# Dilated 3x3 convolution: pair 0 in one transfer beside the weights, and six pairs asked for ahead instead of five

## The chip, the cores and the metric

The kernel runs on one core of a Trainium2 chip. The metric is the device time of one execution in microseconds; the time before is the median of three runs. A core has TensorE (PE, with its weight loads PEld), VectorE (DVE), ScalarE (ACT), GpSimd (POOL) and SyncE (SP), and 16 DMA engines that move data between the chip's memory and the core. SyncE, ScalarE and GpSimd can each ask for transfers, each into a queue of its own; all queues are served by the same 16 DMA engines.

## The reference

The inputs are x (16 images, 64 channels, 64 x 64, float32) and weight (128 x 64 x 3 x 3, float32). The dilation is 2 and the padding is 2, so the output is 16 x 128 x 64 x 64 in float32:

```
x_pad = np.pad(x, ((0, 0), (0, 0), (pad, pad), (pad, pad)))
for b, co, ci, kh, kw:
    output[b, co] += weight[co, ci, kh, kw] * x_pad[b, ci, kh*2:kh*2+64, kw*2:kw*2+64]
```

## The kernel before

**Tiling.** Two images form a pair: their 2 x 64 channels fill the 128 partitions, one row of 64 x 64 float32 (16 KB) on each. There are eight pairs (NP). On TensorE the two images are two matmuls on 64 partitions each, issued in turn.

**The arithmetic.** With dilation 2 the rows fall into groups of four (a quad): two rows of an even class and two of an odd class (e and r in the code). The three rows of weights w0, w1, w2 are regrouped so that fewer matmuls are needed: the sum of the even and odd classes (s16) is multiplied with w1 once and used for both classes, and the differences w2 - w1 and w0 - w1 (slots w21 and w01) and w0 and w2 complete each class. Each pair is done in four units (u) of four quads. A unit has three phases of matmuls: w1 on s16, which ScalarE copies out of PSUM (line 204), and two class phases, which VectorE adds to that copy and writes to the output tile (line 209). The PSUM pool has four buffers.

**Loads.** Pair 0 comes as float32 in two pieces of rows (0 to 35, 36 to 63) from SyncE's queue, into x32, which borrows a slot of the output pool (three slots). VectorE (line 130, rows 0 to 19) and ScalarE (line 132, the rest) convert it to float16, and GpSimd forms s16 from it directly (line 141, `prepare`). All other pairs come through GpSimd's queue, which converts to float16 on the way (line 81, `load`); x16 has six slots. The weights come first in SyncE's queue (line 64), ahead of pair 0.

**Weights.** Two ScalarE copies (line 99) convert them, VectorE and GpSimd form w21 and w01 (line 103), 15 small matmuls transpose them (line 117), and VectorE and ScalarE move the transposed blocks from PSUM to w_sb (lines 126 and 128).

**Order.** The order on each engine is the order in which the code issues; there is no scheduler. On GpSimd it is: first half of w01, load of pair 1, second half of w01, sums of rows 0 to 19 of pair 0, loads of pairs 2, 3 and 4, sums of the other rows of pair 0, and from then on the sums of the next pair within the loop, with the loads of pairs 5, 6 and 7 each ahead of the sums of pairs 4, 5 and 6:

```
if u == 1 and AHEAD <= pb + 2 < NP:
    load(pb + 2, [0, H])
```

**Stores.** SyncE's queue stores pairs 0 to 4 whole (line 221), pairs 5 and 6 per image, and pair 7 per image and half (line 224). An output slot is written again three pairs later, after its store.

Of the kernel before, what the change touches and what calls it, by code (L numbers as in the profile page):

```python
# [10 lines left out]
def kernel(  # L11
# [7 lines left out]
    nc = tc.nc  # L19

    B, CI, H, W = x.shape
# [38 lines left out]
    x_pair = x.rearrange("(nb two) c h w -> nb (two c) h w", two=2)  # L60


    w32 = wpool.tile([CO, CI * NK], f32, name="w32")
    nc.sync.dma_start(out=w32, in_=weight.rearrange("o i h w -> o (i h w)"))  # L64

    x16 = {}
    s16 = {}
# [3 lines left out]
    cuts0 = [0, 20, 36, 52, H]  # L71
    x32 = opool.tile([P, 2, H, W], f32, tag="o", name="x32")[:, 0]
    x16[0] = x16pool.tile([P, H, W], f16, tag="x16", name="x16_0")
    for lo, hi in ((0, 36), (36, H)):
        nc.sync.dma_start(out=x32[:, lo:hi], in_=x_pair[0, :, lo:hi])


    def load(pb, cuts):
        x16[pb] = x16pool.tile([P, H, W], f16, tag="x16", name=f"x16_{pb}")
        for lo, hi in zip(cuts, cuts[1:]):  # L80
            nc.gpsimd.dma_start(out=x16[pb][:, lo:hi], in_=x_pair[pb, :, lo:hi])  # L81

    AHEAD = 5


    zero = wpool.tile([P, NB], f16, name="zero")
# [13 lines left out]
    for name, a in (("w21", 2), ("w01", 0)):  # L100
        for u in range(2):
            eng = nc.vector if name == "w21" else nc.gpsimd
            eng.tensor_sub(  # L103
                out=w16[:, SLOT[name] * KW : (SLOT[name] + 1) * KW, u, :],
# [8 lines left out]
    for n, name in enumerate(("w1", "w21", "w0", "w01", "w2")):  # L113
        ps = cpool.tile([P, 2, NB], f32, tag="ps", name=f"wt{n}")
        k0 = SLOT[name] * KW
        for j in range(KW):
            nc.tensor.matmul(  # L117
                out=ps[:, 0, j * CO : (j + 1) * CO],
# [16 lines left out]
    def prepare(pb, lo, hi):  # L135
        if pb not in s16:
            s16[pb] = sumpool.tile([P, 2 * NQ, W], f16, tag="s16", name=f"s16_{pb}")
        src = (x16[pb] if pb else x32).rearrange("p (q e r) w -> p q e (r w)", e=2, r=2)
        dst = s16[pb].rearrange("p (q r) w -> p q (r w)", r=2)
        q0, q1 = lo // 4, hi // 4  # L140
        nc.gpsimd.tensor_add(  # L141
            out=dst[:, q0:q1], in0=src[:, q0:q1, 0, :], in1=src[:, q0:q1, 1, :]
        )

    prepare(0, 0, 20)
    for pb in range(2, AHEAD):
        load(pb, [0, H])
# [42 lines left out]
    for pb in range(NP):  # L190
        o = opool.tile([P, 2, H, W], f32, tag="o", name=f"o{pb}")
        ov = o.rearrange("p b (q e r) w -> p b q e (r w)", e=2, r=2)
        for u in range(NU):

            if u == 1 and AHEAD <= pb + 2 < NP:
                load(pb + 2, [0, H])
# [8 lines left out]
            for e, terms in enumerate(  # L205
# [4 lines left out]
                    out=ov[:, :, u * UQ : (u + 1) * UQ, e, :],  # L210
# [49 lines left out]
```

## Time and profile before

| | |
|---|---|
| median of three runs | 126.11 us (126.09 to 126.12) |
| profiled execution, first to last instruction (span) | 124.3 us |
| PE busy | 105.2 us (85% of the span) |
| VectorE busy | 80.8 us (65%) |
| GpSimd busy | 41.4 us (33%) |
| ScalarE busy | 39.6 us (32%) |
| read from and written to the chip's memory | 17.07 MB, 33.55 MB |
| weights, issue to landing | 2.9 us |
| pair 0, its two pieces, issue to landing | 6.5 and 10.6 us |
| other pairs, issue to landing, median of seven | 16.0 us |

The page gives the profiled execution by its span; the runs' time holds 1.8 us more than the span, before the first and after the last instruction. In the lists of groups, a line names the source line, the engine, the operation, the tiles out<-in, the shapes, and the number of instructions. The slices cut the span in 40 parts of 3.1 us, and their digits are tenths of busy time. The DMA row is the mean over the 16 DMA engines, and the GB/s are bytes written: a load that converts float32 to float16 writes half of what it reads. "SPq" and "POOLq" are the queues' issuing instructions.

### The profile page before, as it was taken

Reading aid. Unit: us, or ns where it says so; the run is one execution under the profiler, and the core shown is the slowest. Engines: PE = TensorE matmul, PEld = TensorE weight load, DVE = VectorE, ACT = ScalarE, POOL = GpSimd, SP = SyncE. Lnnn points to the kernel's source line nnn. Section 1 sums busy time; section 2 is a strip of 40 time slices with the busy share of each in tenths; the row PEclk is TensorE's granted clock in tenths of the full one; section 3 lists DMA queues with packets and bytes.
Section 4 is the critical chain, followed back from the end, with each engine's and each line's share of the span. In section 5 each row is a group of like instructions: output and inputs, shape, how many; then the busy total and the mean of one; then the engine's idle time right before and its main releaser. Section 6 shows DMA issues by size and latency. Waiting matters only on the chain.

```text
span 124.3 us, 2244 instructions
## 1 busy us (share of the span) xinstructions
PE 105.2 (85%) x981; PEld 55.7 (45%) x981; DVE 80.8 (65%) x71; ACT 39.6 (32%) x40; POOL 41.4 (33%) x33
## 2 busy tenths in 40 slices
PE   6357999999999999999999999999999999960000
PEld 2043555555555555555555555555555555520000
DVE  0470199787778777877769778777877787770000
ACT  4760823333333333333333333333332433320000
POOL 2859998794095009500930093000000000000000
PEclk9999999999999999999999999999999999999655
DMA  4999999999999999999999999999999999999991
GB/s 129 346 359 218 214 214 216 224 237 411 393 327 314 332 306 319 316 390 314 324 345 427 425 427 432 422 427 427 432 438 427 432 414 432 427 417 419 422 406 71
DMA packets 3961, 43.42 MB, mean 349 GB/s; under 512 B 368, under 2 KB 368, under 8 KB 624
## 3 DMA queue, kind: packets, MB, share of 16 engines
q1 hardware_dynamic: 2944, 35.95, 68.9%
q0 software_dynamic: 1008, 7.34, 28.4%
q8 instruction: 7, 0.11, 0.3%
q14 instruction: 2, 0.02, 0.0%
HBM read 17.07 MB, written 33.55 MB: 407 GB/s over the span
## 4 chain that ended last, share of the span: by engine, by line
PE 80%; DMA 5%; POOL 2%; DVE 1%; DVEq 1%; SPq 0%; issue 0%
PE ps L186 80%; DMA x<-in_x_dram 5%; POOL s L141 2%; DVE o L209 1%; DVEq L255 1%; SPq L64 0%; DVEq L209 0%
## 5 line engine op out<-in xcount | busy, mean ns | idle before, releaser
L209 DVE TENSOR_TENSOR o<-ps,s 128x1024 f32<-128x1024 f32 x64 | 76.7, 1223 | 25.9 <-PE ps L186 16.8
L186 PE MATMUL ps<-x,w_sb 64*128 64x496 f16 (+3 forms) x768 | 85.3, 368 | 0.0
L186 PEld LDWEIGHTS <-w_sb 64*128 64x128 f16 x960 | 53.4, 95 | 49.3 <-issue 3.7
L204 ACT COPY s<-ps 128x1024 f32<-128x1024 f32 x32 | 32.4, 1012 | 63.0 <-PE ps L186 63.0
L141 POOL TENSOR_TENSOR s<-x 128x1152 f16<-128x1152 f16 (+4 forms) x18 | 35.1, 1971 | 31.1 <-PE ps L186 28.3
L186 PE MATMUL ps<-s,w_sb 64*128 64x496 f16 (+1 forms) x192 | 26.5, 379 | 2.1 <-POOL s L141 2.1
L81 POOL DMA_DIRECT2D x<-in_x_dram x7 | 4.0, 579 | 0.0
L132 ACT CAST x<-x 128x1024 f16<-128x1024 f32 (+1 forms) x3 | 2.8, 973 | 3.4 <-DMA x<-in_x_dram 3.4
L93 PE MATMUL warm<-zero 128*128 128x512 f16 x6 | 2.7, 630 | 1.2 <-DVE zero L87 1.2
L117 PE MATMUL wt<-ident,w 128*128 128x128 f16 x15 | 1.8, 312 | 2.1 <-ACT w L99 2.1
L103 DVE TENSOR_TENSOR w<-w 128x192 f16<-128x192 f32 x2 | 1.5, 800 | 2.5 <-DMA w<-in_weight_dram 2.5
L117 PEld LDWEIGHTS <-w 128*128 128x128 f16 x15 | 1.5, 146 | 3.0 <-ACT w L99 3.0
L99 ACT CAST w<-w 128x576 f16<-128x576 f32 x2 | 2.3, 1222 | 1.6 <-DMA w<-in_weight_dram 1.6
L103 POOL TENSOR_TENSOR w<-w 128x192 f16<-128x192 f32 x2 | 1.9, 951 | 2.4 <-DMA w<-in_weight_dram 2.4
L126 DVE CAST w_sb<-wt 128x384 f16<-128x384 f32 x3 | 1.6, 552 | 1.4 <-PE wt L117 1.4
L93 PEld LDWEIGHTS <-zero 128*128 128x128 f16 x6 | 0.7, 138 | 2.3 <-DVE zero L87 1.2
L99 ACT ACT_TABLE_LOAD x1 | 1.3, 1283 | 0.7 <-PEq L241 0.7
L128 ACT CAST w_sb<-wt 128x384 f16<-128x384 f32 x2 | 1.0, 478 | 1.1 <-PE wt L117 1.1
L130 DVE CAST x<-x 128x1280 f16<-128x1280 f32 x1 | 0.8, 826 | 0.5 <-DMA x<-in_x_dram 0.5
L87 DVE MEMSET zero<- 128x256 uint32 x1 | 0.3, 272 | 0.9 <-PEq L241 0.9
masks.py:199 POOL TENSOR_SCALAR_AFFINE_SELECT ident<-ident 128x128 f16<-128x128 f16 x1 | 0.3, 292 | 0.1
masks.py:197 POOL MEMSET ident<- 128x128 f16 x1 | 0.2, 204 | 0.3 <-POOLq L241 0.3
(4 smaller groups left out, 0.4 us busy)
## 6 DMA issues: line engine op xcount, KB each, us to landing
out_dram<-o SPq DMA_DIRECT2D x5, 4096.0 KB, 21.6
out_dram<-o SPq DMA_DIRECT2D x4, 2048.0 KB, 12.4
x<-in_x_dram POOLq DMA_DIRECT2D x7, 1024.0 KB, 16.0
out_dram<-o SPq DMA_DIRECT2D x4, 1024.0 KB, 10.6
x<-in_x_dram SPq DMA_DIRECT2D x1, 1152.0 KB, 6.5
x<-in_x_dram SPq DMA_DIRECT2D x1, 896.0 KB, 10.6
w<-in_weight_dram SPq DMA_DIRECT2D x1, 288.0 KB, 2.9
```

Source lines behind the costliest of these rows:

```text
L81: nc.gpsimd.dma_start(out=x16[pb][:, lo:hi], in_=x_pair[pb, :, lo:hi])
L93: nc.tensor.matmul(out=warm[:, 0], lhsT=zero[:, 0:P], rhs=zero, start=True, stop=True)
L99: nc.scalar.copy(out=w16[:, 0:NK, u, :], in_=w32k)
L103: eng.tensor_sub(out=w16[:, SLOT[name] * KW : (SLOT[name] + 1) * KW, u, :], in0=w32k[:, a * KW : (a + 1) * KW, :], in1=w32k[:, KW : 2 * KW ...
L117: nc.tensor.matmul(out=ps[:, 0, j * CO : (j + 1) * CO], lhsT=w16[:, k0 + j, :, :].rearrange("o t i -> o (t i)"), rhs=ident, start=True, st ...
L126: nc.vector.tensor_copy(out=dst, in_=ps[:, 0, 0 : KW * CO])
L132: nc.scalar.copy(out=x16[0][:, lo:hi], in_=x32[:, lo:hi])
L141: nc.gpsimd.tensor_add(out=dst[:, q0:q1], in0=src[:, q0:q1, 0, :], in1=src[:, q0:q1, 1, :])
L186: nc.tensor.matmul(**m)
L204: nc.scalar.copy(out=s32, in_=phase(pb, u, [("w1", 2, 0)]))
L209: nc.vector.tensor_add(out=ov[:, :, u * UQ : (u + 1) * UQ, e, :], in0=ps.rearrange("p b (q c) -> p b q c", c=QW), in1=s32.rearrange("p b ( ...
L255: with _tile.TileContext(nc) as tc:
```

## The change

The weights are asked for from ScalarE's queue instead of SyncE's. Pair 0 is one transfer of 64 rows per partition (2 MB) instead of two of 36 and 28 rows, and stands first in SyncE's queue. AHEAD goes from 5 to 6: the load of pair 5 follows those of pairs 2, 3 and 4 ahead of the first unit, and the loop loads only pairs 6 and 7. The cuts in which pair 0 is converted and summed stay.

```
     w32 = wpool.tile([CO, CI * NK], f32, name="w32")
-    nc.sync.dma_start(out=w32, in_=weight.rearrange("o i h w -> o (i h w)"))
+    nc.scalar.dma_start(out=w32, in_=weight.rearrange("o i h w -> o (i h w)"))
...
     x16[0] = x16pool.tile([P, H, W], f16, tag="x16", name="x16_0")
-    for lo, hi in ((0, 36), (36, H)):
-        nc.sync.dma_start(out=x32[:, lo:hi], in_=x_pair[0, :, lo:hi])
+    nc.sync.dma_start(out=x32, in_=x_pair[0])
...
-    AHEAD = 5
+    AHEAD = 6
```

## The prediction

> **What bounds the kernel now.** I read the page's slices first, for what runs without a break; then the chain that ended last, the issues of transfers with their landings, GpSimd's timeline, and the start in stretches of half a microsecond. From the page:
>
> ```profile
> span 124.3 us, 2244 instructions
> ...
> PE   6357999999999999999999999999999999960000
> ...
> DMA  4999999999999999999999999999999999999991
> ...
> HBM read 17.07 MB, written 33.55 MB: 407 GB/s over the span
> ```
>
> Two resources run nearly the whole time: PE from slice 6 to 36, and the 16 DMA engines from slice 2 to the end. The packet records of the trace bear out the second: first packet at 1.74 us, last at 122.6, and the packets' durations add up to 121.3 us per engine, so there is no idle DMA time to win. The span is 124.3 us; the median of the runs, 126.11, is 1.8 above it, which I take as constant around the span. I sum shifts of the span's end and add them to 126.11.
>
> ```profile
> 1.17 6.48 DMA x<-in_x_dram
> 7.65 0.07 issue
> 7.72 2.19 POOL s L141
> ...
> 9.95 99.61 PE ps L186 x948
> ...
> 109.66 1.23 DVE o L209
> ```
>
> The chain: the first piece of pair 0 lands at 7.65, GpSimd adds its rows, PE starts at 9.95 and doesn't stop. The chain stops at VectorE, 12 us before the end: behind it are only stores, which still drain. The issues, from the page, last column issue to landing:
>
> ```profile
> x<-in_x_dram SPq DMA_DIRECT2D x1, 1152.0 KB, 6.5
> x<-in_x_dram SPq DMA_DIRECT2D x1, 896.0 KB, 10.6
> w<-in_weight_dram SPq DMA_DIRECT2D x1, 288.0 KB, 2.9
> ```
>
> The weights, first in SyncE's queue, land at 0.74 + 2.9 = 3.6. GpSimd's timeline shows what hangs on them:
>
> ```profile
> 3.69 1.10 POOL L103 TENSOR_TENSOR w<-w 128x192 f16<-128x192 f32 x1 [2.38 <-DMA w<-in_weight_dram]
> 4.74 0.70 POOL L81 DMA_DIRECT2D x<-in_x_dram  x1
> 5.46 0.80 POOL L103 TENSOR_TENSOR w<-w 128x192 f16<-128x192 f32 x1
> 7.72 2.18 POOL L141 TENSOR_TENSOR s<-x 128x640 f16<-128x640 f32 x1 [1.47 <-DMA x<-in_x_dram]
> 9.84 1.63 POOL L81 DMA_DIRECT2D x<-in_x_dram  x3
> ```
>
> The load of pair 1 stands in GpSimd's order behind a subtraction that waits for the weights. Windows of 0.5 us (last columns: DMA share, GB/s written):
>
> ```profile
> 7.50:8.00 0.50, 0.32 (x3) 0.15 (x2) 0.32 (x1) 0.46 (x2) 0.28 (x1) 1.00 1.09 459
> 8.00:8.50 0.50, 0.00 (x0) 0.00 (x0) 0.50 (x2) 0.50 (x2) 0.50 (x1) 1.00 1.39 408
> 8.50:9.00 0.50, 0.00 (x0) 0.00 (x0) 0.50 (x3) 0.46 (x1) 0.50 (x1) 1.00 0.94 180
> ```
>
> The rate halves at 8.5: loads that convert write half of what they read. The first of their packets starts at 8.24, 3.5 us after the issue at 4.74, and just as most engines finish pair 0. That hand-over has no gap.
>
> **The change, part by part.** *Pair 0 in one transfer.* Removed: one issue on SyncE (0.42 us), 128 packets. Each DMA engine carries 8 rows: 8 x (0.347 + 0.272) = 4.95 us now, 8 x 0.611 (the stores' packet of a whole 16 KB row) = 4.89 after: 0.06 saved. But rows 0 to 19 are now usable only when all rows have landed.
>
> *Weights on ScalarE's queue.* Their issue (0.37) goes ahead of, or behind, the table load (0.74 to 2.02). ScalarE idles 1.62 us before its first weight copy, so the issue costs nothing by itself, but the order "weights, then x" is gone; both transfers use the same 16 engines. How two queues share an engine the trace shows where the slowest two engines still hold rows of pair 0 while conversion loads are queued: their 7 KB packets start at 9.28, 10.16 and 11.05, steps of 0.88 to 0.89 = 0.272 + 0.624, one packet of each in turn. The weights are 8 packets of 0.093 per engine; in turn with 0.611 they need eight steps, 8 x 0.704 = 5.63 us, as long as pair 0 itself. From 1.74 that is 7.4. Slow packets add 0.84 (means now 126, 411 and 280 ns against medians 93, 347 and 272, times 8), so 8.2; the slowest engine was 1.3 later in the first piece (last packet 6.99 against some 5.6), so 9.5; landing followed the last packet by 0.35. Pair 0 lands at 9.9, the weights one row earlier, at **9.2 instead of 3.6**. Bounds: 3.6 (all weight packets first) and 9.9 (behind the rows).
>
> *What the weights hold up.* GpSimd's order stays: subtraction, issue of pair 1 at weights + 1.13, first packet 3.5 later, 9.2 + 4.63 = 13.8. For those 3.5 there are two rows: this one, and 4.6 for the load of pair 5 (28.77 to 33.34) beside stores; I take the first, the same instruction in the same place, and keep both. DMA engines finish pair 0 at 8.5 on the mean, the slowest at 9.5 without the interleaving. So they idle 5.3 us on the mean, 4.3 on the slowest. Nothing else can fill this: the next transfer of another queue is the store of pair 0 at 25.45 plus the delay. As no idle DMA time lies behind it, it moves the end. The final semaphores arrived at 123.37 from the slowest engine, and the first below the two slowest at 122.71: 122.71 + 5.3 = 128.0 against 123.37 + 4.3 = 127.7, so **+4.6**, less 0.06.
>
> *PE.* GpSimd finishes its weight work at weights + 2.65 = 11.85, adds the rows in 2.19, and PE starts at 14.1, 4.1 later. The path through ScalarE is shorter: copies 2.34, transposes and VectorE's eviction done 3.5 after the weights. Is a PE that is 4.1 late worse than a DMA that is 4.6 late? The store of pair 6 is issued at 99.75, starts at 101.74, and the one before ends at 101.7: its slack is what exceeds the shortest issue-to-packet time, between 1.0 (first issue) and 2.0, so 0 to 1.0, take 0.5. PE's delay counts 3.6, inside the 4.6.
>
> *Six pairs ahead.* One more issue (0.55) on GpSimd between the first rows and rows 20 to 35: those were ready at 12.75, PE wanted them at 14.54, so 1.8 covers it; without that cover it would cost the 0.55. Pair 5's load moves from the issue at 28.77 to right behind pair 4's. The DMA total is the same, and by 29 stores fill the engines: zero. It delays the first stores, though: VectorE waits once, 1.23 us at 62.5, for the store of pair 1 to free its buffer. Sharing engines half and half, I put that store's end 5.8 later, 1.7 more than PE's delay, so that wait becomes some 2.9. PSUM's four buffers hid 1.23 wholly; up to 1.0 may reach PE, 4.1 + 1.0 - 0.5 = 4.6: the same end.
>
> Sum: 126.11 + 4.6 - 0.06 = **130.7**.
>
> **Rivals.** *Weights get through first.* If ScalarE's transfer reaches the engines some 0.4 us ahead (one issue's length), three or four packets go alone, and the weights land near 5.9; in one go, at 3.6. Then conversion loads start between 8.2 and 10.5, the DMA gap shifts the end by at most 122.71 + 2.0 - 123.37 = 1.3, and pair 0's landing rules: 9.9 + 0.07 + 2.2 = 12.2, PE 2.2 late, less 0.5 of slack: +1.7, **127.8**. For it: the two engines leave the opening barrier together. Against: SyncE's first issue starts as early as any (0.74), and alternating from the start already gives my case. The Trainium skill, DMA: Bandwidth & Descriptors, section "Queues, rings and completion order", says that an engine drains a whole packet, typically 9 to 17 descriptors, before it turns to another queue. By that rule all eight weight rows would pass in one go, landing at 3.6 or behind pair 0 at 9.9, for 127.8 or 131.4; the steps of 0.88 us above speak for one row at a time.
>
> *A gain in the slowest engine (the other side).* The lag of 1.3 us arises among the slow packets of the first 7 us. If one transfer of whole rows had none, and the weights passed early, all would land at 1.74 + 5.63 + 0.35 = 7.7, PE starts as before, loads follow at 8.24, and the last engine ends up to 1.3 earlier: **124.8**. It decides only if pair 0 lands before 8.2 and the weights before 4.0; the first 2 MB took until 8.5 even on the mean engine. The Trainium skill's section "Anatomy of one DMA — SWDGE (gpsimd) path" on the same page gives each transfer a fixed cost of about 2.0 us. By it one transfer less would land pair 0 2.0 us sooner, an estimate from that page; but the second piece's packets start at 5.91, before the first's last at 6.99, so here nothing fixed stood between them.
>
> *No change:* the landing is hidden, with pair 0 at 8.5 (mean engine) and the weights by 4: PE starts at 10.8, 0.8 late, which the upper bound of the slack (1.0) takes in, and loads follow at 8.6: **126.1**.
>
> **How the numbers follow.** Late weights 0.70, weights first 0.20, no change 0.05, gain 0.05. The likeliest has its own range: weights from 7.1 (1.74 + 8 x 0.704 - 0.61 + 0.35, no slow packet) give loads at 11.8 and +2.6, 128.7; weights at 9.9 with 4.6 to the first packet give loads at 15.6 and +6.4, 132.5. With the rival at 127.8 the range is 127.4 to 132.3. What a measurement here can tell from no change is 0.2%, 0.25 us: faster 0.05, same 0.05, slower 0.90.
>
> **What would show it.** Right: GpSimd's and VectorE's waits for the weights grow from 2.4 to some 8 us; pair 1's issue near 10.3; a hole of 4 to 5 us in the DMA slices before 14; PE's first convolution near 14, its run still 99.6 long or up to 1 longer; stores dense to the end. Wrong: weights landed by 6 (then the start is ruled by pair 0 and PE), a DMA hole that other transfers fill, or a tail with idle DMA between the last stores, which would mean that PE and not DMA sets the end.

## The result, and the profile after

The changed kernel takes 131.25 us (131.01 to 131.40), the kernel before 126.12 beside it: a ratio of 1.037, with a 95% interval of 1.0335 to 1.0405. The change costs 5.1 us. The profiled execution took 131.2, with a span of 129.4 against 124.3, so the 1.8 us around the span stayed. Medians are over all executions of a kernel; ranges and ratios leave out those that were disturbed.

The page of the changed kernel (slices of 3.2 us, tenths of busy time):

```profile
span 129.4 us, 2241 instructions
...
PE   6203999999999999999999999999999999950000
...
DMA  4953999999999999999999999999999999999991
...
HBM read 17.07 MB, written 33.55 MB: 391 GB/s over the span
```

The bytes are the same, but the DMA row has a dip at slices 3 and 4, which the row of before lacks: a hole, in which the DMA engines stand idle. Behind it the row is dense to the end, as it was. Windows of the changed kernel over the hole (each line: the stretch and its length, the busy time of PE, PEld, VectorE, ScalarE and GpSimd, the granted clock, and last the DMA share and the GB/s written; before, the DMA share was 1.05, 1.01 and 1.10 in these windows):

```profile
8.00:10.00 2.00, 0.00 (x0) 0.00 (x0) 0.59 (x2) 0.59 (x1) 0.54 (x1) 1.00 0.13 51
10.00:12.00 2.00, 0.20 (x3) 0.20 (x4) 0.92 (x1) 1.75 (x2) 1.98 (x4) 1.00 0.22 25
12.00:14.00 2.00, 2.00 (x19) 1.55 (x19) 1.66 (x2) 1.17 (x3) 2.00 (x3) 1.00 0.82 123
```

The cause stands in the issues and in GpSimd's order. Issues of the changed kernel, last column issue to landing:

```profile
x<-in_x_dram SPq DMA_DIRECT2D x1, 2048.0 KB, 8.4
w<-in_weight_dram ACTq DMA_DIRECT2D x1, 288.0 KB, 8.7
```

GpSimd's timeline of the changed kernel (start, length, engine, line, operation, what ended the idle time before it):

```profile
9.46 1.11 POOL L102 TENSOR_TENSOR w<-w 128x192 f16<-128x192 f32 x1 [8.15 <-DMA w<-in_weight_dram]
10.51 0.70 POOL L80 DMA_DIRECT2D x<-in_x_dram  x1
11.23 0.80 POOL L102 TENSOR_TENSOR w<-w 128x192 f16<-128x192 f32 x1
11.98 1.53 POOL L140 TENSOR_TENSOR s<-x 128x640 f16<-128x640 f32 x1
13.46 2.46 POOL L80 DMA_DIRECT2D x<-in_x_dram  x4
```

The weights, asked for at 0.73, land at 9.38 instead of 3.6, pair 0 lands whole at 9.18, and pair 1's load is issued at 10.51 instead of 4.74. Nothing is left in any queue from 8.7 until that load's first packet at 11.94.

The chain that ended last (start, length, what):

```profile
0.73 8.65 DMA w<-in_weight_dram
...
9.41 2.35 ACT w L98 x2
...
11.80 1.78 PE wt L116 x15
13.59 55.19 PE ps L185 x516
...
68.88 1.24 DVE o L208
...
70.16 43.64 PE ps L185 x420
...
113.89 1.22 DVE o L208
```

The start now runs through ScalarE's weight copies, and there is a break at 68.8: PE waits for a free PSUM buffer, because VectorE waited there. VectorE's timeline shows it:

```profile
68.88 3.48 DVE L208 TENSOR_TENSOR o<-ps,s 128x1024 f32<-128x1024 f32 x3 [2.42 <-PE ps L185]
```

The profile names PE as releaser, but pair 1's store, whose buffer the next output tile takes, has its last landing at 68.76, just before: it was the store.

### The profile page after: what moved, and what is told of

Read it like the earlier page. It is cut to its first block, busy times and chain, and to the rows that moved or that the text cites. A ratio compares the mean times of both kernels' runs of the same rounds, so it can differ in the third digit from the quotient of the medians.

```text
span 129.4 us, 2241 instructions
## 1 busy us (share of the span) xinstructions
PE 105.7 (82%) x981; PEld 56.0 (43%) x981; DVE 81.4 (63%) x71; ACT 39.5 (31%) x40; POOL 41.0 (32%) x33
## 4 chain that ended last, share of the span: by engine, by line
PE 78%; DMA 7%; DVE 2%; ACT 2%; DVEq 1%; issue 0%
PE ps L185 76%; DMA w<-in_weight_dram 7%; DVE o L208 2%; ACT w L98 2%; PE wt L116 1%; DVEq L254 1%; DVEq L208 0%
## 5 line engine op out<-in xcount | busy, mean ns | idle before, releaser
L140 POOL TENSOR_TENSOR s<-x 128x1152 f16<-128x1152 f16 (+4 forms) x18 | 34.4, 1939 | 30.0 <-PE ps L185 28.5
L129 DVE CAST x<-x 128x1280 f16<-128x1280 f32 x1 | 1.4, 1392 | 0.0
```

The costliest lines, as they stand in the source:

```text
L129: nc.vector.tensor_copy(out=x16[0][:, 0:20], in_=x32[:, 0:20])
L140: nc.gpsimd.tensor_add(out=dst[:, q0:q1], in0=src[:, q0:q1, 0, :], in1=src[:, q0:q1, 1, :])
```

## The account of the DMA engines

In the packet records of the trace the durations, summed and divided by the 16 engines, give a busy time. What is left between the first packet (at 1.74 in both) and the end of the last is idle time and the lag of the slowest engine; as records overlap a little, it can come out just below zero. (The prediction's 122.6 is where the last row packet starts; it ends at 122.9.)

| profiled execution | busy | last packet ends | left over |
|---|---|---|---|
| before | 121.3 | 122.9 | -0.2 |
| changed | 122.3 | 128.0 | 4.0 |

Left over is 4.1 us more (0.6 of it before 9 us, 3.4 from 9 to 14), busy 0.9 more, together the 5.1 by which the last packet ends later. The 0.9 is slow packets: pair 1's load, the first behind the hole, averages 712 ns a packet instead of 632 (0.64 us per engine), and the loads of pairs 4 and 5 add 0.54 near 32 us, where the first store joins; pair 0 itself gives 0.14 back. That pair 1's packets are slow because of the hole is not shown: in four runs below that have pair 0 in one transfer and no hole ahead of this load they average 661 to 702.

PE's delay is not what sets the end here. Pair 6's store was issued at 103.91 and its first packet went at 106.67, 2.77 later, while 0.83 is the shortest such time of this store in any run (below): it stood in a queue. PE's last matmul came 4.2 later than before; the DMA engines were later still.

## The experiments

Theory A is that of the prediction: weights in turns with pair 0's rows, a late load of pair 1, and a hole that moves the end. The rivals are the whole-row transfer, the sixth pair, and the late PE. "Before" is the median beside each run, on the same chip.

**Weights first again**, in the changed kernel:

```
-    nc.scalar.dma_start(out=w32, in_=weight.rearrange("o i h w -> o (i h w)"))
+    nc.sync.dma_start(out=w32, in_=weight.rearrange("o i h w -> o (i h w)"))
```

> The changed kernel with the weights put back first in SyncE's queue; pair 0 stays one transfer and six pairs stay ahead. Theory A (the weights, slowed by pair 0's rows, issue pair 1's load late, and the DMA engines stand idle): weights at 3.6, no DMA hole, pair 0 at 8.5 to 9.5, PE from 10.7 to 11.5, time 126.0 to 127.1. Theory B (the whole-row transfer or the sixth pair is what costs): 129 or more.

128.29 (127.35 to 129.04) against 126.53, ratio 1.0135 (1.0065 to 1.0206). The hole is gone (packets of pair 1 from 7.87), and with it some 3 us of the 5.1. But the time is above what theory A expected, and this kernel's chain (start, length, what) shows the whole-row landing:

```profile
1.17 8.34 DMA x<-in_x_dram
...
9.58 2.18 POOL s L140
...
11.80 100.58 PE ps L185 x948
```

So the order of the weights is the larger part, not the whole. Part of the rest is slow packets without a hole: in this trace the DMA engines' busy time is 122.95, 1.6 more than before (pair 1's packets average 681 ns, pair 2's 677, pair 5's 752).

**Pair 0 held back, weights still on ScalarE's queue**, in the changed kernel:

```
-    nc.sync.dma_start(out=x32, in_=x_pair[0])
...
     nc.vector.memset(zero, 0.0)
+    nc.vector.memset(x32[:, 0:1, 0:1], 0.0)
+    nc.sync.dma_start(out=x32, in_=x_pair[0])
```

> The changed kernel with pair 0's transfer held back about 0.6 us by a tiny VectorE write into its tile, so that the weights of the other queue reach the engines first. Theory A: most weight rows pass alone, weights at 3.6 to 5, pair 0 at 9 to 9.5, no hole, 126.2 to 127.3. If a second queue as such costs: 131.

128.01 (127.66 to 128.02) against 126.46, ratio 1.0154 (1.0051 to 1.0258): above the expectation again, equal to the run above within the intervals. The weights land at 3.54 from ScalarE's queue. A second queue as such costs nothing that can be seen; a start 0.45 us earlier than pair 0's is enough.

**Two pieces again, weights still on ScalarE's queue**, in the changed kernel:

```
-    nc.sync.dma_start(out=x32, in_=x_pair[0])
+    for lo, hi in ((0, 36), (36, H)):
+        nc.sync.dma_start(out=x32[:, lo:hi], in_=x_pair[0, :, lo:hi])
```

> The changed kernel with pair 0 in two pieces again; weights on ScalarE's queue, six pairs ahead. Theory A, with the trace's one-for-one turns: the weights' rows alternate with rows of 9 KB, eight steps of 0.347 + 0.093 = 3.5 us behind the slow first packet, weights at 6.3 to 7.0 instead of 9.4, a DMA hole of 1 to 2.5 us, time 127.4 to 129. If the single transfer were the cause: 126.1. If the size of the other queue's rows did not matter: 131.

129.00 (128.95 to 129.29) against 126.53, ratio 1.0200 (1.0159 to 1.0240). The size of the other queue's rows counts: with rows of 9 KB in place of 16 KB the weights land at 7.20, between 3.6 and 9.38, and pair 1 is issued at 8.32, in this kernel's timeline of GpSimd:

```profile
7.28 1.11 POOL L103 TENSOR_TENSOR w<-w 128x192 f16<-128x192 f32 x1 [5.96 <-DMA w<-in_weight_dram]
8.32 0.70 POOL L81 DMA_DIRECT2D x<-in_x_dram  x1
```

The hole is some 1 us long; the first packet behind it starts at 9.73.

**Weights on ScalarE's queue as the only change to the kernel before:**

```
-    nc.sync.dma_start(out=w32, in_=weight.rearrange("o i h w -> o (i h w)"))
+    nc.scalar.dma_start(out=w32, in_=weight.rearrange("o i h w -> o (i h w)"))
```

> The kernel before with the weights on ScalarE's queue alone (pair 0 in two pieces, five pairs ahead). Weights near 7.2, pair 1's issue near 8.3, a hole of 1 to 1.5 us with slow packets behind it: 128.3 to 129.3, as with six pairs ahead.

128.90 (128.68 to 129.72) against 126.50, ratio 1.0206 (1.0144 to 1.0268): the same as with six pairs ahead (129.00).

**One transfer as the only change to the kernel before:**

```
-    for lo, hi in ((0, 36), (36, H)):
-        nc.sync.dma_start(out=x32[:, lo:hi], in_=x_pair[0, :, lo:hi])
+    nc.sync.dma_start(out=x32, in_=x_pair[0])
```

> The kernel before with pair 0 in one transfer alone (weights first in SyncE's queue, five pairs ahead). Pair 0 lands near 9 and PE starts near 11.3 to 11.8, no hole. If the whole-row landing costs by itself, as the weights-first run suggests: 127.2 to 128.5. If that run's extra time came from the sixth pair: 126.1 to 126.7.

128.44 (127.92 to 128.55) against 126.50, ratio 1.0145 (1.0098 to 1.0191). It costs 1.8 by itself, with the weights at 3.59 and no hole. Two things come with it, of like size. PE starts at 11.9, 1.95 late. And the DMA engines' busy time is 123.0, 1.7 more than before: 0.2 in pair 1's packets, 0.6 in pair 2's, whose load GpSimd now issues at 11.80 instead of 9.84, 1.4 before pair 1's packets run out, and 1.0 in the first store's, near 33 us. Pair 6's store waited 1.36 from issue to first packet, 0.5 more than the shortest: both limits were near. Which of the two decides stays open. The first store's packets are slow (681 to 683 ns on the mean, 620 in the profiled execution of before) in three profiles, here, with five pairs ahead and with PE late alone; in these three its first packet goes 0.90 to 0.96 after the issue, so it hardly waited, and in every other profile 1.5 or more. Why such packets are slow stays open.

**Five pairs ahead in the changed kernel:**

```
-    AHEAD = 6
+    AHEAD = 5
```

> The changed kernel with five pairs ahead instead of six. Theory A: the hole stays, 131.0 to 131.4, and PE's stall of about 0.5 us near 69 us goes because the store of pair 1 ends earlier. If the earlier load of pair 5 takes part in the cost by way of that stall: 130.6 or less.

131.94 (131.07 to 132.09) against 126.53, ratio 1.0413 (1.0361 to 1.0465): not faster. PE's stall near 69 us is gone, as expected. What that is worth alone this run can't say, as two costs came with it: the slow packets of the first store (681 ns on the mean, 1.0 us per engine), and a new wait that no expectation held, of PE for w_sb at 15, because VectorE's conversion of rows 0 to 19 ran 2.41 us beside GpSimd (0.83 before, 1.39 in the changed kernel; 2.40 in the run with the weights on ScalarE's queue alone, which shows the same wait). From this kernel's timeline:

```profile
12.77 2.41 DVE L129 CAST x<-x 128x1280 f16<-128x1280 f32 x1
...
15.70 4.89 PE L185 MATMUL ps<-x,w_sb 64*128 64x512 f16 x24 [0.73 <-DVE w_sb L125]
```

**Six pairs ahead as the only change to the kernel before:**

```
-    AHEAD = 5
+    AHEAD = 6
```

> The kernel before with six pairs ahead alone. Theory A: no idle DMA time, the same work, 125.9 to 126.4; VectorE's wait for the store of pair 1 grows from 1.2 us to 2 to 3. If the sixth pair costs by way of that wait: 126.6 or more.

126.63 (126.51 to 127.41) against 126.53, ratio 1.0003 (0.9966 to 1.0039): no difference. VectorE's wait for pair 1's store did not grow, against what theory A said of it: no two of its additions start more than 2.1 us apart here, and 2.44 lay across that wait before. This execution also had PE start early, at 9.15, without being faster.

**A hole alone.** In the kernel before, pair 1's load goes behind the sums of rows 0 to 19:

```
-            if name == "w01" and u == 0:
-                load(1, [0, H])
...
-    for pb in range(2, AHEAD):
+    for pb in range(1, AHEAD):
```

> The kernel before with pair 1's load moved behind the sums of rows 0 to 19: a DMA hole without late weights and without a late PE (PE from 9.9 or a little earlier). Theory A (idle DMA time moves the end one for one): issue near 9.9, first packet 1.4 us later, hole of some 2.8 us and slow packets behind it, 128.7 to 129.8. Theory C (the late PE sets the end): 126.1.

130.03 (129.53 to 130.15) against 126.46, ratio 1.0252 (1.0177 to 1.0327), 3.2 us more by the ratio, with the weights as early as before and pair 0 in two pieces. A hole is enough to move the end; theory C's 126.1 (the late PE sets it) is excluded. By which way is less clear. The one profiled execution took 131.53 and lies outside the range. In it the first packet goes 1.41 after the issue at 10.95, and left over is 3.8; but PE started at 11.05, 1.1 late instead of on time (1.3 late cost 1.4 in the next run), and later stood still for 3.2, as this kernel's timeline shows:

```profile
70.08 3.49 DVE L207 TENSOR_TENSOR o<-ps,s 128x1024 f32<-128x1024 f32 x3 [5.50 <-DMA out_dram<-o]
71.36 2.69 PE L184 MATMUL ps<-x,w_sb 64*128 64x512 f16 x12 [3.21 <-DVE o L207]
```

VectorE waited for pair 1's store, and PE for VectorE; the granted clock then reads 0.50 from 70.81 to 74.22. Pair 6's store then went 0.91 after its issue, so PE was close to setting the end there. Whether the faster executions have such a stall is not shown.

**PE late alone.** In the kernel before, the loads of pairs 2 to 4 go ahead of the first sums, and those sums are done twice:

```
-    prepare(0, 0, 20)
     for pb in range(2, AHEAD):
         load(pb, [0, H])
+    prepare(0, 0, 20)
+    prepare(0, 0, 20)
```

> The kernel before with the loads of pairs 2 to 4 ahead of the first sums, and those sums done twice (the second writes the same values), so that PE starts at 12.3, 2.4 late, while the DMA engines have no hole. By my reckoning with a slack of 0 to 1.0 for PE: 127.4 to 128.5. If DMA alone sets the end: 126.1. If PE's delay counts in full: 128.5.

127.91 (127.30 to 128.93) against 126.46, ratio 1.0110 (1.0071 to 1.0150). PE started at 11.2 and not 12.3, as each sum took 1.56 and not 2.18, but its slow first stretch lasted longer and its last matmul came 2.5 late. Inside the expected range, but not by the expected way: 1.0 us of slow packets with the first store is in this trace too, and ahead of that store (issued at 27.99, first packet at 28.90) the DMA engines stand idle for 0.8 us per engine: the loads asked for ahead had run out before it came. So with five pairs ahead a late PE can open a hole of its own at the first store, and this run does not separate the two limits.

**No hole, and PE far behind.** In the changed kernel, all five loads ahead of the subtractions:

```
+    for pb in range(1, AHEAD):
+        load(pb, [0, H])
     for name, a in (("w21", 2), ("w01", 0)):
...
-            if name == "w01" and u == 0:
-                load(1, [0, H])
...
-    for pb in range(2, AHEAD):
-        load(pb, [0, H])
```

> The changed kernel with all five loads of pairs 1 to 5 issued by GpSimd ahead of the weights' subtractions: the DMA engines never idle, but three queues take turns, so the weights need eight steps of 0.611 + 0.093 + 0.624 = 10.6 us: they land at 12 to 13.5, PE starts near 17, 7 late. If the larger of the two delays sets the end (DMA 0, PE 7 less 0.5): 131.8 to 133.5. If the hole alone is the cost: 126.1.

129.33 (128.62 to 130.30) against 126.46, ratio 1.0215 (1.0128 to 1.0301): above 126.1 and below 131.8, so neither expectation. The weights land at 11.83 and PE starts 6 us late, yet the end moves by 2.5 in the profiled execution. Here PE rules: the DMA engines run dry ahead of pair 6's store, whose first packet goes 0.83 after its issue at 104.64. Two lines of this kernel's chain, and the window around that issue (DMA share 0.70):

```profile
0.74 11.10 DMA w<-in_weight_dram
...
16.04 98.50 PE ps L183 x938
```

```profile
100.00:106.00 6.00, 6.00 (x64) 2.86 (x60) 4.76 (x5) 2.02 (x2) 0.00 (x0) 1.00 0.70 294
```

Three things soften the delay. Pair 6's store waited 1.99 before against 0.83 here, so 1.16 was queueing, PE's real slack. The engines also finish together here, after running dry: the last store's 16 landings spread from 125.65 to 125.89, and from 120.87 to 123.37 before, where the slowest engine ends 2.5 behind the first. And PE ran 99.3 instead of 100.4 from its first convolution matmul to its last, as its start at half pace (last section) took 1.2 and not 3.1.

**The hole filled, the weights still late.** In the changed kernel:

```
+    idle = wpool.tile([P, NB], f16, name="idle")
+    for _ in range(5):
+        nc.gpsimd.tensor_add(out=idle, in0=zero, in1=zero)
+    load(1, [0, H])
     for name, a in (("w21", 2), ("w01", 0)):
...
-            if name == "w01" and u == 0:
-                load(1, [0, H])
```

> The changed kernel with pair 1's load ahead of the weights' subtractions on GpSimd, held back by five idle additions (some 5 us) so that its rows arrive about when pair 0's are done: the hole is filled, the weights stay as late (9.4 to 10.2), and PE starts as late (13.3 to 14.5). If the hole sets the end of the changed kernel, what is left is PE's delay of some 4 less its slack of 1 to 2: 127.5 to 129.2. If the late PE sets it: 131.

The changed kernel itself was run again beside it:

> The changed kernel once more, beside its variants on one chip: 131.0 to 131.9.

129.57 (129.34 to 129.71) against 131.23 (131.14 to 131.57) for the changed kernel beside it, and 126.50 before: ratios 1.0246 (1.0211 to 1.0281) and 1.0384 (1.0348 to 1.0420). PE starts at 13.58 here and 13.51 there, and the weights land at 9.45 and 9.32; only the DMA engines differ at the start. Windows of the kernel with the hole filled, as above:

```profile
8.00:10.00 2.00, 0.00 (x0) 0.00 (x0) 0.53 (x2) 0.53 (x1) 0.47 (x1) 1.00 0.94 156
10.00:12.00 2.00, 0.13 (x2) 0.14 (x3) 0.98 (x1) 1.81 (x2) 2.00 (x3) 1.00 0.98 205
```

With the same late PE, 1.7 us come back, so the late PE doesn't set the changed kernel's end. It is less than theory A's 2 to 3.7, and 129.57 lies above the expected 127.5 to 129.2. The account says why: left over falls from 3.9 to 1.3, but busy grows from 122.5 to 123.1, since the loads of pairs 2 to 5 wait behind the weights and come when pair 1's packets have run out: another hole of 0.7 us near 14 us, with 0.9 of slow packets in pair 2's load. In both kernels the late weights open a hole where the next load stands behind them.

None of these versions beats the kernel before; six pairs ahead alone equals it.

## Why the prediction was right

The forecast was 130.7 (127.4 to 132.3), slower with a chance of 0.90; measured 131.25.

- **What bounds the kernel**: held for the changed kernel. Its DMA engines are busy to the end, pair 6's store waits for them, and 1.7 us came back when the hole was filled with PE as late. It is not a rule: with PE 6 us late, PE set the end.
- **Weights at 9.2**: 9.38. In the changed kernel's records an engine's rows of pair 0 start at 4.169, 4.865, 5.562 and 6.258 us, steps of 0.696 to 0.697 (0.704 by the sum of the two rows), with one weight row in each step. The Trainium skill, DMA: Bandwidth & Descriptors, section "Queues, rings and completion order", has an engine drain a packet, typically 9 to 17 descriptors, from one queue before it turns to the next. Counted in rows the trace differs, one row in turn, and the measurement decides; how many descriptors a row is, the records don't say. The turns were right, but the sum behind 9.2 was not: no engine was 1.3 late (the last row of pair 0 ends at 8.67, not 9.5), the landing followed the last weight packet (8.75) by 0.63 instead of 0.35, and the weights landed after pair 0 (9.18), not a row before it. These errors cancel.
- **First packet of pair 1's load 3.5 after its issue**: the mis-sized term. It was 1.43 here (10.51 to 11.94), 1.40 to 1.42 in the other runs where the queues stood empty (8.32 to 9.73, 10.46 to 11.86). The 3.5 and 4.6 of before were taken from busy engines. The Trainium skill, same page, section "Specifications", gives about 1 us to the first byte on this path; the trace, counted from the start of the issue, comes near it for idle queues only.
- **A hole of 5.3 on the mean engine**: 3.4 from 9 to 14 us, too long by the term above.
- **Terms at nothing or taken off**: the slow packets behind the hole and where the first store joins, 0.9 us of busy time, where the forecast had counted slow packets at the start alone; 0.6 of idle time before 9 us; and 0.7 that the forecast took off because the slowest engine would catch up, which it didn't (the last store's landings still spread over 2.5 us, 125.91 to 128.44). Together these outweigh the 1.9 by which the hole was too long: the last packet ends 5.1 later, against the forecast's 4.6. The way from the weights to the hole to the end was right; that the number came so close is partly luck.
- **PE at 14.1**: 13.57. GpSimd's sums took 1.53 and not 2.18, and so ended together with the way through ScalarE, at 13.5.
- **Six pairs ahead cost nothing, with a longer wait of VectorE and up to 1.0 us of PE stall**: VectorE's wait was 2.42 (forecast 2.9), PE's run was 0.6 longer (100.2 against 99.6), and six pairs ahead alone left the kernel before at the same time.
- **The rival "weights get through first", 127.8**: forced in two runs, 128.29 and 128.01. The price was near; its reason, pair 0's landing alone, is not settled, as slow packets have a like share.
- **The rival with a gain, 124.8**: nothing of it came. The fixed cost of 2.0 us that it weighs is given in the Trainium skill's section for GpSimd's path, while pair 0 goes through SyncE's queue. So what the prediction works out from it settles nothing for this case.
- **Slack of PE 0.5 (0 to 1.0)**: 1.16 for pair 6's store, and more where a lagging engine catches up. My expectation of 131.8 for PE 6 us late failed on this.
- **The range**: its upper end of 132.3 lies below the prediction's own bound of 132.5, without a reason given; the result doesn't hang on it.

## What to carry over

Where the DMA engines are busy to the end, look for what the next load stands behind in its issuing engine's order: a small transfer that this order waits for must be ahead of the large ones, as here each of its rows waited out one row of the other queue, and the larger those rows, the longer. Account with busy time and left-over time per DMA engine before blaming the late compute engine; and look for holes in the middle too, as a late first store can open one. A first piece is worth its extra transfer if something starts on it: one transfer in place of two cost 1.8 us by itself.

## What the runs showed of the hardware

- A load issued by GpSimd starts 1.4 us after the issue on idle DMA engines, and 4.4 to 4.6 beside stores (42.28 to 46.89, 54.67 to 59.11 in the changed kernel). Beside the rows of pair 0 it was 1.66 with the hole filled (6.73 to 8.39), 3.1 to 3.7 in the kernels with early weights, and 4.87 with all loads first (1.42 to 6.29): that the engines are busy does not settle it, and what does is open.
- Pair 1's packets average 712 to 742 ns behind a hole, against 625 to 632 without one where pair 0 comes in two pieces: 0.7 to 0.9 us per engine above the usual 0.625 a packet. A hole is not the only companion: with pair 0 in one transfer they average 661 to 702 without a hole (weights first, pair 0 held back, one transfer alone, hole filled), and 624 with all loads first.
- VectorE's conversion of 128 x 1280 elements took 0.83, 1.39 and 2.41 us in three executions, with GpSimd at work beside it; what exactly slows it was not tried.
- PE starts its convolutions at half pace, pairs of matmuls 0.41 us apart instead of 0.21, for 3.1 us before, 3.8 in the changed kernel, and 5.4 in the run with six pairs ahead alone. There PE began 0.8 us earlier than before and its last matmul was 0.2 later. The granted clock goes with it: in that run it reads 0.50 from 7.63 to 14.46, and the pace rises at 14.56. The other traces have no clock record before the rise, so the 1.00 that the profile prints there is not a reading; their first record, of the full clock, comes within 0.2 us of the rise (at 13.18 and 13.04 before, at 17.43 and 17.39 in the changed kernel).
